# A two-layer decoder trunk: decay matrices and the D·x term moved to ScalarE, eight conditioning chunks moved from GpSimd to TensorE

## The chip, the cores and the metric

The kernel runs on one core of one Trainium2 chip. The metric is the device time of one execution in microseconds. A core has five engines, each with its own in-order queue: TensorE (PE, matrix products; PEld is its weight load), VectorE (DVE), ScalarE (ACT), GpSimd (POOL) and SyncE (SP, which here only issues DMAs). An instruction at the head of a queue that waits for another engine or for a DMA holds everything behind it on that queue. Instructions of different engines meet through semaphores.

## The reference, cut to what matters

512 tokens of width 1024 pass through two layers. All data are float32. The change touches layer 0's state-space part and its conditioning vector:

```python
cs = silu(c)
mod = cs @ ada_w[i] + ada_b[i]                    # 6*1024 values per layer: sh1, sc1, g1, sh2, sc2, g2
h = rms_norm(x, g) * (1 + sc1) + sh1
z, xbc, dt_raw, q, k, v = split(h @ w_in)
xbc = silu(causal_conv4(xbc)); xs, B, C = split(xbc)
a_cs = cumsum(dt * A)                             # within chunks of 128 tokens
decay = exp(where(causal, a_cs[l] - a_cs[s], -inf))
y_diag = einsum(((C @ B^T) * decay), xs * dt)     # per chunk, 32 heads of 64, 4 groups of 8 heads
y_off  = (C @ carried_state) * exp(a_cs)          # the state is carried from chunk to chunk
y = rms_norm((y_diag + y_off + D * xs) * silu(z)) # D is d_skip, one number per head
x = x + g1 * (concat(y, attention) @ w_out)
x = x + g2 * swiglu(rms_norm(x) * (1 + sc2) + sh2)
```

Layer 1 (a Conformer convolution and a second SwiGLU) and the final norm aren't touched.

## The kernel before, in words

**Products.** Activations lie with features on the 128 partitions and 512 tokens along the row. To keep float32 accuracy every weight and activation is split into a high part in a rounded type and the rest (`slab`, L179 to L196: the weight arrives by DMA in `raw`, ScalarE casts the high part `whi`, and the engine named by `eng` subtracts to get the low part `wlo`), and `products` (L198 to L211) adds three matmul passes: high·high (L207), low·high (L208), high·low (L210). `raw`, `whi` and `wlo` have two buffers each, so the next weight's DMA waits for the subtraction of the weight two before.

**Order.** The functions are written in program order, but the framework's scheduler lists the instructions of each engine's queue in an order of its own, from its estimates of when operands are ready. The queue is then fixed: at run time each engine goes through it in order.

**The state-space stage.** It runs from about 40 us to 415 us. For each of four groups, `ssm_inputs(g)` projects B, C (`wbc`, results `bc`), four x tiles (`wx`) and four z tiles (`wz`), through two PSUM banks named `pj` that are used in turn. `conv_tile` (L440) empties a bank: one ScalarE instruction (L443) and three VectorE ones (L446) that read PSUM, then a tanh (L449) and a product (L450). A bank is free again only after the last L446. `ssm_group(g)` then treats four chunks of 128 tokens: a broadcast DMA brings `ar` (eight heads by 128 positions of `a_cs`, on all partitions), GpSimd subtracts the per-partition `acs` (L487), VectorE takes the minimum with 0 (L488), ScalarE the exponential (L489), VectorE multiplies with the masked `cb` (L500), and TensorE forms `pd` (L504). From the second chunk on, `po` (L516) brings the carried state's part, times `ef` (exponential of another broadcast DMA, L513, L514); VectorE joins the two into `y1` (L517, L518). `pst` (L526) and `prev` (L529 to L532) carry the state; `btok` (L522), a ScalarE copy, feeds `pst`. After the four chunks VectorE adds D·x (L536), z is multiplied in (L537), and `ystat` collects squares. `ar` has two buffers, so the DMA for chunk c waits until `pd` of chunk c-2 has read its tile.

**Conditioning.** `mod` is needed in columns of 128. Sixteen chunks are made ahead of the stage by VectorE (`ada_wide`). The other 32 (`ada_pool`, L165 to L173) are made by GpSimd one at a time: a DMA of 128 columns, a product with `cs` (L170), three halving additions (L172), and a TensorE transpose with a VectorE sum (L153, L155, L156). Of these, eight are written behind each of groups 0 and 1, and the last 16 in the attention stage, three behind each head pair.

**Low parts in group 0.** `SL = (G, G, G, G)` (L179) gives the low parts of the dt, B/C and x weights of group 0 to GpSimd.

Of the kernel before, what the change touches and what calls it, by code (L numbers as in the profile page):

```python
# [9 lines left out]
F32 = mybir.dt.float32  # L10
F32R = mybir.dt.float32r
I32 = mybir.dt.int32
AF = mybir.ActivationFunctionType
ALU = mybir.AluOpType
# [3 lines left out]
P = 128  # L18
# [4 lines left out]
KT = D // P  # L23
# [3 lines left out]
GROUPS = 4  # L27
HEADS = 32
HPG = HEADS // GROUPS
# [48 lines left out]
def trunk_kernel(ctx: ExitStack, tc, a, out, dbg=None):  # L78
    nc = tc.nc
    V, S, G, PE = nc.vector, nc.scalar, nc.gpsimd, nc.tensor  # L80
# [5 lines left out]
    tmp = ctx.enter_context(tc.tile_pool(name="tmp", bufs=2))  # L86
# [3 lines left out]
    def bank(tag, name, shape=(P, T)):  # L90
        return psum.tile(list(shape), F32, tag=tag, name=name)
# [6 lines left out]
    ones = const.tile([P, P], F32, name="ones")  # L98
# [33 lines left out]
    cs = const.tile([P, KT], F32, name="cs")  # L132
# [11 lines left out]
    adab = [pa[:, 16:64], None]  # L144
# [3 lines left out]
    mod = [const.tile([P, 48], F32, name="mod0"), None]  # L148
# [9 lines left out]
    def ada_wide(pool, tag, l, j0, ws):  # L158
# [3 lines left out]
            V.scalar_tensor_tensor(acc, ws[k // 4][:, k % 4, :], cs[:, k:k + 1], acc, op0=ALU.mult, op1=ALU.add)  # L162
        return ada_finish(l, acc, j0, 4)

    def ada_pool(pool, bufs, l, j):  # L165
        w = pool.tile([P, 1024], F32, tag="adaw", name=f"adap{l}_{j}", bufs=bufs)
        G.dma_start(w.rearrange("p (k c) -> p k c", k=KT),
                          a["ada_w"][l][:, j * P:(j + 1) * P].rearrange("(k p) c -> p k c", p=P))
        w3 = w.rearrange("p (k c) -> p k c", k=KT)
        G.tensor_tensor(w3, w3, cs.unsqueeze(2).broadcast_to([P, KT, P]), op=ALU.mult)  # L170
        for n in (512, 256, 128):
            G.tensor_tensor(w[:, 0:n], w[:, 0:n], w[:, n:2 * n], op=ALU.add)  # L172
        ada_finish(l, w, j, 1)  # L173
# [2 lines left out]
        return [(l, j) for j in range(lo, hi)]  # L176


    SL = (G, G, G, G)  # L179

    def slab(parts, name, eng=V):

# [270 lines left out]
    def ssm_inputs(g):  # L453
# [19 lines left out]
                zs.append(z)  # L473
        return bt, ct, xs, zs

    ystat = Stat("ys", 16)

    def ssm_group(g, bt, ct, xs, zs):
        y1 = ssm.tile([P, 4, T], F32, tag="y1", name=f"y1_{g}", bufs=1)
        prev = None  # L480
        for c in range(NB):
            n = f"{g}_{c}"
            cl = slice(c * P, (c + 1) * P)
            hs = slice(c * HEADS + g * HPG, c * HEADS + (g + 1) * HPG)
            ar = ssm.tile([P, HPG, P], F32, tag="ar", name="ar" + n)
            nc.sync.dma_start(ar, a_dram[g * HPG:(g + 1) * HPG, c, :].unsqueeze(0).broadcast_to([P, HPG, P]))
            G.tensor_tensor(ar, ar, acs[:, hs].unsqueeze(2).broadcast_to([P, HPG, P]), op=ALU.subtract)  # L487
            V.tensor_scalar(ar, ar, 0.0, None, op0=ALU.min)  # L488
            S.activation(ar, ar, AF.Exp)  # L489
            px = bank(TB[0], "px" + n)  # L490
            for t in range(4):
                PE.transpose(px[:, t * P:(t + 1) * P], xs[t][:, cl], ident)
            xdt = ssm.tile([P, HPG, 64], F32, tag="xdt", name="xdt" + n)
            V.tensor_tensor(xdt, px.rearrange("p (h d) -> p h d", d=64),
                            dt[:, hs].unsqueeze(2).broadcast_to([P, HPG, 64]), op=ALU.mult)
            pb = bank(TB[1], "pb" + n, (P, 2 * P))
            PE.matmul(pb[:, 0:P], bt[:, cl], ct[:, cl], start=True, stop=True)
            cb = ssm.tile([P, P], F32, tag="cb", name="cb" + n)
            V.tensor_tensor(cb, pb[:, 0:P], tri, op=ALU.mult)
            V.tensor_tensor(ar, ar, cb.unsqueeze(1).broadcast_to([P, HPG, P]), op=ALU.mult)  # L500
            pd = bank(TB[2], "pd" + n)
            for hh in range(HPG):
                o = (hh % 2) * 64
                PE.matmul(pd[o:o + 64, (hh // 2) * P:(hh // 2 + 1) * P], xdt[:, hh, :], ar[:, hh, :],  # L504
                          start=True, stop=True)
            if c == 0:
                S.copy(y1[:, :, cl], pd.rearrange("p (t l) -> p t l", l=P))
            else:
                po = bank(TB[3], "po" + n)
                ef = ssm.tile([P, 4, P], F32, tag="xe", name="ef" + n, bufs=3)  # L510
                for e in range(2):
                    src = a_dram[g * HPG + e:(g + 1) * HPG:2, c, :]
                    nc.sync.dma_start(ef[e * 64:(e + 1) * 64], src.unsqueeze(0).broadcast_to([64, 4, P]))  # L513
                S.activation(ef, ef, AF.Exp)  # L514
                for t in range(4):
                    PE.matmul(po[:, t * P:(t + 1) * P], prev[:, 2 * t:2 * t + 2, :], ct[:, cl], start=True, stop=True)  # L516
                V.tensor_tensor(y1[:, :, cl], po.rearrange("p (t l) -> p t l", l=P), ef, op=ALU.mult)  # L517
                V.tensor_tensor(y1[:, :, cl], pd.rearrange("p (t l) -> p t l", l=P), y1[:, :, cl], op=ALU.add)  # L518
            if c < NB - 1:
                PE.transpose(pb[:, P:2 * P], bt[:, cl], ident)  # L520
                btok = ssm.tile([P, P], F32, tag="btok", name="btok" + n)
                S.copy(btok, pb[:, P:2 * P])  # L522
                xde = ssm.tile([P, HPG, 64], F32, tag="xe", name="xde" + n, bufs=3)
                G.tensor_tensor(xde, xdt, dend[:, hs].unsqueeze(2).broadcast_to([P, HPG, 64]), op=ALU.mult)
                pst = bank(TB[4], "pst" + n)
                PE.matmul(pst, btok, xde.rearrange("p h d -> p (h d)"), start=True, stop=True)  # L526
                new = ssm.tile([P, HPG, 64], F32, tag="prev", name="prev" + n)
                if c == 0:
                    S.copy(new, pst.rearrange("p (h d) -> p h d", d=64))  # L529
                else:  # L530
                    G.tensor_tensor(new, prev, cdec[:, hs].unsqueeze(2).broadcast_to([P, HPG, 64]), op=ALU.mult)
                    V.tensor_tensor(new, pst.rearrange("p (h d) -> p h d", d=64), new, op=ALU.add)  # L532
                prev = new
        for t in range(4):
            ft = 4 * g + t
            V.scalar_tensor_tensor(y1[:, t, :], xs[t], dsk[:, ft:ft + 1], y1[:, t, :], op0=ALU.mult, op1=ALU.add)  # L536
            (V if g == GROUPS - 1 else G).tensor_tensor(y1[:, t, :], y1[:, t, :], zs[t], op=ALU.mult)  # L537
            ystat.add(y1[:, t, :])
        nc.sync.dma_start(yd_dram[4 * g:4 * g + 4].rearrange("t p l -> p t l"), y1)

    jobs = [(0, j) for j in range(16, 48)]

    def ada_some(pool, bufs, n):
        for _ in range(min(n, len(jobs))):
            ada_pool(pool, bufs, *jobs.pop(0))
# [15 lines left out]
    nc.sync.dma_start(b_dram, bv)  # L561
    for g in range(GROUPS):
        ssm_group(g, *ins)
        if g < GROUPS - 2:
            ada_some(ssm, 2, 8)
        if g + 1 < GROUPS:
            ins = ssm_inputs(g + 1)
    ctx_s.close()
# [524 lines left out]
```

## Time and profile before

| | |
|---|---|
| time, median of 3 runs | 1872.89 us (1870.29 to 1874.12) |
| profiled execution | 1885.09 us, span 1882.8 us |
| PE busy | 1774.7 us, 94% |
| DVE busy | 1046.5 us, 56% |
| ACT busy | 693.1 us, 37% |
| POOL busy | 430.5 us, 23% |
| mean granted TensorE clock | 0.972 |
| chain that ended last | PE 73%, DVE 11%, DMA 7%, ACT 3%, POOL 2% |

The profiled execution is 12 us longer than the median run. "Busy" is a sum over the whole span, so it hides that the stages differ. The stage views below (busy time of each engine between two times) separate them. PE busy counts a matmul from its start to its modelled end; matmuls overlap, so the time that one takes from its neighbours is read from the distance between starts.

### The profile page before, as it was taken

Reading aid. Unit: us, or ns where it says so; the run is one execution under the profiler, and the core shown is the slowest. Engines: PE = TensorE matmul, PEld = TensorE weight load, DVE = VectorE, ACT = ScalarE, POOL = GpSimd, SP = SyncE. Lnnn points to the kernel's source line nnn. Section 1 sums busy time; section 2 is a strip of 40 time slices with the busy share of each in tenths; the row PEclk is TensorE's granted clock in tenths of the full one; section 3 lists DMA queues with packets and bytes.
Section 4 is the critical chain, followed back from the end, with each engine's and each line's share of the span. In section 5 each row is a group of like instructions: output and inputs, shape, how many; then the busy total and the mean of one; then the engine's idle time right before and its main releaser. Section 6 shows DMA issues by size and latency. Waiting matters only on the chain.

```text
span 1882.8 us, 24868 instructions
## 1 busy us (share of the span) xinstructions
PE 1774.7 (94%) x9735; PEld 1450.0 (77%) x9735; DVE 1046.5 (56%) x1978; ACT 693.1 (37%) x1331; POOL 430.5 (23%) x328
## 2 busy tenths in 40 slices
PE   5897978999999999997999999999999999999998
PEld 3676766777778878777888888897567988888888
DVE  7858687755565565558665664373204743333336
ACT  6333333334545454344421221253214632122225
POOL 1437686422443440003000000013020200000001
PEclk8998989999999999997999999999998999999999
DMA  8354454545444443424555553253640523322223
GB/s 301 102 138 140 141 141 134 137 112 152 123 128 149 133 125 122 124 74 141 181 190 190 188 201 114 79 169 80 180 132 1 169 77 102 101 89 93 87 94 130
DMA packets 232066, 247.84 MB, mean 132 GB/s; under 512 B 13946, under 2 KB 198076, under 8 KB 231949
## 3 DMA queue, kind: packets, MB, share of 16 engines
q1 hardware_dynamic: 220813, 204.31, 36.6%
q0 software_dynamic: 11136, 41.95, 6.8%
q8 instruction: 77, 1.26, 0.3%
q14 instruction: 40, 0.33, 0.1%
HBM read 228.73 MB, written 8.64 MB: 126 GB/s over the span
## 4 chain that ended last, share of the span: by engine, by line
PE 73%; DVE 11%; DMA 7%; ACT 3%; issue 2%; POOL 2%; SPq 1%; DVEq 0%; ACTq 0%; POOLq 0%
PE fd L207 4%; PE fd L208 4%; PE fd L210 4%; PE fg L208 4%; PE fg L207 4%; PE fu L207 4%; PE fu L208 4%; PE fu L210 4%; PE fg L210 4%; PE cps L959 2%; PE s L717 2%; DMA ar<-a_dram 2%; PE wa L207 1%; PE wa L208 1%; PE wa L210 1%
## 5 line engine op out<-in xcount | busy, mean ns | idle before, releaser
L249 POOL TENSOR_TENSOR n_acc<-n_acc,n_q 128x256 f32<-128x256 f32 x32 | 29.7, 929 | 561.8 <-ACT n_q L245 561.7
L207 PE MATMUL fd<-uh,wd_h 128*128 128x512 f32 (+1 forms) x448 | 148.6, 347 | 0.9 <-DVE xT L592 0.9
L195 DVE TENSOR_TENSOR wf_l<-wf_w,wf_h 128x1024 fp32r<-128x1024 f32 x88 | 106.1, 1241 | 74.4 <-ACT wf_h L194 74.4
L208 PE MATMUL fd<-uh,wd_l 128*128 128x512 f32 (+1 forms) x448 | 147.0, 344 | 0.0
L194 ACT CAST wf_h<-wf_w 128x1024 fp32r<-128x1024 f32 x88 | 87.7, 1048 | 115.7 <-PE fd L210 71.9
L208 PE MATMUL fg<-n_h,wf_l 128*128 128x512 f32 x320 | 126.1, 394 | 2.0 <-DVE wf_l L195 2.0
L207 PE MATMUL fg<-n_h,wf_h 128*128 128x512 f32 x320 | 126.3, 395 | 0.7 <-ACT wf_h L194 0.5
L208 PE MATMUL fu<-n_h,wf_l 128*128 128x512 f32 x320 | 124.7, 390 | 0.0
L207 PE MATMUL fu<-n_h,wf_h 128*128 128x512 f32 x320 | 124.6, 389 | 0.0
L172 POOL TENSOR_TENSOR adap<-adap 128x128 f32<-128x128 f32 (+2 forms) x96 | 103.5, 1082 | 4.7
L869 DVE TENSOR_TENSOR fs<-fs,fu 128x512 f32<-128x512 f32 x40 | 27.5, 688 | 130.2 <-PE fu L210 130.2
L743 ACT ACTIVATE s<-s,nm 128x128 f32<-128x128 f32 x192 | 79.4, 415 | 50.7 <-DVE nm L739 40.4
L194 ACT CAST wd_h<-wd_w 128x1024 fp32r<-128x1024 f32 (+1 forms) x64 | 57.1, 941 | 101.2 <-PE fd L210 80.6
L592 DVE SCALAR_TENSOR_TENSOR xT<-fd,mod,xT 128x512 f32<-128x512 f32 (+1 forms) x64 | 39.1, 615 | 98.1 <-PE fd L210 97.8
L207 PEld LDWEIGHTS fd<-uh,wd_h 128*128 128x128 f32 x448 | 84.1, 188 | 12.0 <-DVE xT L592 1.3
L208 PEld LDWEIGHTS fd<-uh,wd_l 128*128 128x128 f32 x448 | 84.2, 188 | 10.5
L210 PE MATMUL fd<-ul,wd_h 128*128 128x512 f32 (+1 forms) x448 | 91.9, 343 | 0.0
L170 POOL TENSOR_TENSOR adap<-adap,cs 128x1024 f32<-128x1024 f32 x32 | 67.6, 2112 | 90.3 <-DMA adap<-in_ada_w 90.2
L195 DVE TENSOR_TENSOR wd_l<-wd_w,wd_h 128x1024 fp32r<-128x1024 f32 (+1 forms) x64 | 67.7, 1090 | 34.7 <-ACT wd_h L194 34.4
L162 DVE SCALAR_TENSOR_TENSOR adaa<-adaw,cs,adaa 128x512 f32<-128x512 f32 x112 | 84.8, 758 | 2.6
L210 PEld LDWEIGHTS fd<-ul,wd_h 128*128 128x128 f32 x448 | 72.9, 188 | 10.6
L210 PE MATMUL fg<-n_l,wf_h 128*128 128x512 f32 x320 | 79.1, 389 | 0.0
(400 smaller groups left out, 4584.5 us busy)
## 6 DMA issues: line engine op xcount, KB each, us to landing
adaw<-in_ada_w POOLq DMA_DIRECT2D x24, 1024.0 KB, 5.7
wf_w<-in_ffn_w_gate SPq DMA_DIRECT2D x22, 1024.0 KB, 5.2
wf_w<-in_ffn_w_up SPq DMA_DIRECT2D x22, 1024.0 KB
adap<-in_ada_w POOLq DMA_DIRECT2D x32, 512.0 KB, 5.5
wd_w<-in_ffn_w_down SPq DMA_DIRECT2D x16, 1024.0 KB, 5.1
wd_w<-in_ffn_w_down SPq DMA_DIRECT2D x16, 768.0 KB, 4.6
wa_w<-in_hy_w_out SPq DMA_DIRECT2D x20, 512.0 KB, 4.1
u<-cu SPq DMA_DIRECT2D x128, 67.5 KB, 2.0
```

Source lines behind the costliest of these rows:

```text
L162: V.scalar_tensor_tensor(acc, ws[k // 4][:, k % 4, :], cs[:, k:k + 1], acc, op0=ALU.mult, op1=ALU.add)
L170: G.tensor_tensor(w3, w3, cs.unsqueeze(2).broadcast_to([P, KT, P]), op=ALU.mult)
L172: G.tensor_tensor(w[:, 0:n], w[:, 0:n], w[:, n:2 * n], op=ALU.add)
L194: S.copy(hi[:, s:e], raw[:, s:e])
L195: eng.tensor_tensor(lo[:, s:e], raw[:, s:e], hi[:, s:e].bitcast(F32), op=ALU.subtract)
L207: PE.matmul(ps[:, cols], hi[:, o(k):o(k) + P], xh, start=k == 0, stop=False)
L208: PE.matmul(ps[:, cols], lo[:, o(k):o(k) + P], xh, start=False, stop=False)
L210: PE.matmul(ps[:, cols], hi[:, o(k):o(k) + P], acts[k][1][:, cols], start=False, stop=k == nk - 1)
L592: V.scalar_tensor_tensor(xT[m][:, cols], ps[:, cols], mod[l][:, go + m:go + m + 1], xT[m][:, cols], op0=ALU.mult, op1=ALU.add)
L717: marks[hp, 0] = marks[hp, 1] = PE.matmul(ps[:, o:o + 2 * wd].rearrange("p (e w) -> p e w", e=2), q, k, start=True, stop=True)
L743: S.activation(s[:, o:o + wd], s[:, o:o + wd], AF.Exp, bias=nm, accum_out=l)
L959: PE.matmul(ps[g * 32:(g + 1) * 32, :], w4[k][:, g * 8 + m, :], u4[k][:, g, t:t + w], start=m == 0, stop=m == 7)
```

## The change: three moves

- **Decay.** `ar` is no longer subtracted on GpSimd and clamped on VectorE. ScalarE forms Relu(acs - ar), head by head in eight instructions of 128x128 (the bias is one number per partition, so it differs by head), and then exp of the negative.
- **D·x.** ScalarE writes D·x into `y1` before the chunks; VectorE adds `pd` to it in every chunk (before: a ScalarE copy of `pd` in the first chunk, an addition in the others), and GpSimd adds `po`·`ef`. The four VectorE additions at the group's end are gone.
- **Conditioning and low parts.** Chunks 16 to 23 are made by TensorE (`ada_rows`): eight 128x512 weight tiles through three buffers, each multiplied with a stationary operand of 32 columns of which one is `cs`, into one of four 32-row quarters of a PSUM bank; a ScalarE copy; four products with ones that add the rows. Chunks 24 to 47 all go to the attention stage on GpSimd, still three per head pair, so all eight pairs have some (before, the 16 there were used up in the sixth). The low parts of group 0's B/C and x weights go to VectorE.

```diff
+    def ada_rows(pool, l, j0):
+        ps = bank("C", f"adar{l}_{j0}")
+        for k in range(KT):
+            w = pool.tile([P, 512], F32, tag="adaw", name=f"adaw{l}_{j0}_{k}", bufs=3)
+            nc.sync.dma_start(w, a["ada_w"][l][k * P:(k + 1) * P, j0 * P:j0 * P + 512])
+            PE.matmul(ps[k % 4 * 32:(k % 4 + 1) * 32, :], cs32[:, k, :], w, start=k < 4, stop=k >= 4)
+        rw = tmp.tile([P, 512], F32, tag="st_sq", name=f"adas{l}_{j0}")
+        S.copy(rw, ps)
+        pm = bank("C", f"adac{l}_{j0}", (P, 4))
+        for j in range(4):
+            PE.matmul(pm[:, j:j + 1], rw[:, j * P:(j + 1) * P], ones[:, 0:1], start=True, stop=True)
+        V.tensor_tensor(mod[l][:, j0:j0 + 4], pm, adab[l][:, j0:j0 + 4], op=ALU.add)
...
-    SL = (G, G, G, G)
+    SL = (G, V, V, V)
...
+    cs32 = ssm.tile([P, KT, 32], F32, name="cs32", bufs=1)
+    V.memset(cs32, 0.0)
+    V.tensor_copy(cs32[:, :, 0], cs)
...
         y1 = ssm.tile([P, 4, T], F32, tag="y1", name=f"y1_{g}", bufs=1)
+        for t in range(4):
+            S.mul(y1[:, t, :], xs[t], dsk[:, 4 * g + t:4 * g + t + 1])
...
-            G.tensor_tensor(ar, ar, acs[:, hs].unsqueeze(2).broadcast_to([P, HPG, P]), op=ALU.subtract)
-            V.tensor_scalar(ar, ar, 0.0, None, op0=ALU.min)
-            S.activation(ar, ar, AF.Exp)
+            for hh in range(HPG):
+                S.activation(ar[:, hh, :], ar[:, hh, :], AF.Relu, scale=-1.0, bias=acs[:, hs.start + hh:hs.start + hh + 1])
+            S.activation(ar, ar, AF.Exp, scale=-1.0)
...
-            if c == 0:
-                S.copy(y1[:, :, cl], pd.rearrange("p (t l) -> p t l", l=P))
-            else:
+            V.tensor_tensor(y1[:, :, cl], pd.rearrange("p (t l) -> p t l", l=P), y1[:, :, cl], op=ALU.add)
+            if c > 0:
...
-                V.tensor_tensor(y1[:, :, cl], po.rearrange("p (t l) -> p t l", l=P), ef, op=ALU.mult)
-                V.tensor_tensor(y1[:, :, cl], pd.rearrange("p (t l) -> p t l", l=P), y1[:, :, cl], op=ALU.add)
+                V.tensor_tensor(ef, po.rearrange("p (t l) -> p t l", l=P), ef, op=ALU.mult)
+                G.tensor_tensor(y1[:, :, cl], ef, y1[:, :, cl], op=ALU.add)
...
-            ft = 4 * g + t
-            V.scalar_tensor_tensor(y1[:, t, :], xs[t], dsk[:, ft:ft + 1], y1[:, t, :], op0=ALU.mult, op1=ALU.add)
...
-    jobs = [(0, j) for j in range(16, 48)]
+    jobs = [(0, j) for j in range(24, 48)]
...
-        if g < GROUPS - 2:
-            ada_some(ssm, 2, 8)
+        if g < 2:
+            ada_rows(ssm, 0, 16 + 4 * g)
```

The scheduler lists all queues anew. Line numbers of the changed kernel are 14 to 18 higher. On ScalarE, this stood between the first chunk of group 0 and the group's third (`wx_0_h` is a weight cast for group 1, `sb` the emptying of the bank of group 1's B):

```order
L194 CAST wx_0_h<-wx_0_w 128x1024 x2
L507 COPY y_0_843<-pd_0_861 128x4x128
L529 COPY prev_0_878<-pst_0_876 128x512
L514 ACTIVATE ef_2_954<-ef_2_954 128x512
L489 ACTIVATE ar_2_927<-ar_2_927 128x1024
L522 COPY btok_1_918<-pb_1_892 128x128
L443 ACTIVATE sb_1169<-bc_0_1119,cbh,cwh 128x512
```

Now the same place reads (`sc` is the bank of group 1's C, the `ar_0` at the end is group 1's first chunk):

```order
L507 ACTIVATE ar_2_947<-ar_2_947,acs 128x128 x8
L532 ACTIVATE ef_2_981<-ef_2_981 128x512
L508 ACTIVATE ar_2_947<-ar_2_947 128x1024
L540 COPY btok_1_938<-pb_1_911 128x128
L457 ACTIVATE sb_1152<-bc_0_1102,cbh,cwh 128x512
L463 ACTIVATE th_1157<-sb_1152 128x512
L540 COPY btok_2_992<-pb_2_965 128x128
L507 ACTIVATE ar_3_1001<-ar_3_1001,acs 128x128 x8
L508 ACTIVATE ar_3_1001<-ar_3_1001 128x1024
L532 ACTIVATE ef_3_1035<-ef_3_1035 128x512
L507 ACTIVATE ar_0_1449<-ar_0_1449,acs 128x128 x8
L457 ACTIVATE sc_1160<-bc_1_1103,cbh,cwh 128x512
```

The eight Relu instructions of a chunk stand ahead of `btok` and of the instructions that empty the projection banks, and they are the first on ScalarE to need the `ar` DMA.

On VectorE, at the end of group 0 (`cb_0`, `ar_0` and the `sx` from `x_1_0` belong to group 1), before:

```order
L450 SCALAR_TENSOR_TENSOR sx_1251<-th_1256,sx_1251 128x512
L536 SCALAR_TENSOR_TENSOR y_0_843<-sx_608,dsk,y_0_843 128x512
L536 SCALAR_TENSOR_TENSOR y_0_843<-sx_616,dsk,y_0_843 128x512
L536 SCALAR_TENSOR_TENSOR y_0_843<-sx_682,dsk,y_0_843 128x512
L536 SCALAR_TENSOR_TENSOR y_0_843<-sx_690,dsk,y_0_843 128x512
L488 TENSOR_SCALAR ar_1_1498<-ar_1_1498 128x1024
L499 TENSOR_TENSOR cb_0_1476<-pb_0_1474,cst 128x128
L446 SCALAR_TENSOR_TENSOR sx_1317<-x_1_0_1267,cwh,sx_1317 128x511
```

and now:

```order
L209 TENSOR_TENSOR wz_0_l<-wz_0_w,wz_0_h 128x1024
L464 SCALAR_TENSOR_TENSOR sx_1234<-th_1239,sx_1234 128x512
L518 TENSOR_TENSOR cb_0_1469<-pb_0_1467,cst 128x128
L460 SCALAR_TENSOR_TENSOR sx_1300<-x_1_0_1250,cwh,sx_1300 128x511
L519 TENSOR_TENSOR ar_0_1449<-ar_0_1449,cb_0_1469 128x1024
```

The four D·x additions and the clamp are gone from in front of `cb_0` and the bank-emptying `sx`.

On TensorE, behind the third chunk of group 0 (`bc` and `x` are the projections of group 1), before:

```order
L504 MATMUL pd_2_944<-ar_2_927,xdt_2_937 64x128 x8
L516 MATMUL po_2_953<-sc_542,prev_1_924 128x128 x4
L526 MATMUL pst_2_969<-xde_2_967,btok_2_965 128x512
L497 MATMUL pb_3_986<-sc_542,sb_534 128x128
L153 MATMUL ada_16_1036<-cst,adap_16_1030 128x128
L208 MATMUL x_0_0_1193<-n_h_242,wx_0_l 128x512
```

and now:

```order
L523 MATMUL pd_2_970<-ar_2_947,xdt_2_963 64x128 x8
L534 MATMUL po_2_980<-sc_545,prev_1_944 128x128 x4
L544 MATMUL pst_2_996<-xde_2_994,btok_2_992 128x512
L516 MATMUL pb_3_1019<-sc_545,sb_537 128x128
L171 MATMUL adar_16_1060<-adaw_16_0_1061,cs_474 32x512
L171 MATMUL adar_16_1060<-adaw_16_1_1064,cs_474 32x512
L171 MATMUL adar_16_1060<-adaw_16_2_1067,cs_474 32x512
L225 MATMUL bc_1_1103<-n_l_309,wbc_h 128x512
```

The eight quarter-column products of a set stand as three, three, one and one in the queue, the second three 25 projection products, `pd_3` and `po_3` behind the first. The chunk now comes one C product and three x products earlier among the projections.

## Rows read from the trace of the kernel before

**Rows 1.** Stages: us, length, busy PE, PEld, DVE, ACT, POOL, then granted clock
```profile
95.00:415.00 320.00, 286.02 (x1472) 227.23 (x1471) 228.39 (x278) 111.15 (x161) 185.35 (x130) 0.94 0.49 132
440.00:860.00 420.00, 403.84 (x2154) 323.75 (x2154) 238.01 (x697) 190.91 (x544) 114.36 (x92) 0.98 0.43 123
1000.00:1150.00 150.00, 150.00 (x672) 123.65 (x671) 91.22 (x122) 34.90 (x42) 8.98 (x12) 1.00 0.55 182
148.00:151.00 3.00, 3.00 (x9) 2.28 (x8) 3.00 (x6) 0.54 (x1) 2.84 (x3) 0.52 0.31 65
```

**Rows 2.** Waits of PE, 95 to 415 us: total, times, longest
```profile
PE z L207 <- DVE sx L446: 12.1, 2, 9.0
PE pb L520 <- DVE cb L499: 5.3, 1, 5.3
PE pb L497 <- DVE xdt L494: 4.1, 2, 3.2
PE ada L153 <- POOL adap L172: 3.8, 1, 3.8
PE pst L526 <- ACT btok L522: 3.4, 2, 2.4
```

**Rows 3.** Waits of PE, 40 to 95 us
```profile
PE x L207 <- DVE sc L446: 4.3, 1, 4.3
PE x L208 <- POOL wx_l L195: 4.0, 2, 3.3
```

**Rows 4.** DVE groups by line, 95 to 415 us: busy, mean ns, idle before
```profile
L500 DVE TENSOR_TENSOR ar<-ar,cb 128x1024 f32<-128x1024 f32 x16 | 24.2, 1514 | 0.6 <-ACT ar L489 0.5
L195 DVE TENSOR_TENSOR wz_l<-wz_w,wz_h 128x1024 fp32r<-128x1024 f32 x14 | 22.6, 1612 | 0.0
L488 DVE TENSOR_SCALAR ar<-ar 128x1024 f32<-128x1024 f32 x16 | 20.1, 1257 | 23.0 <-POOL ar L487 23.0
L536 DVE SCALAR_TENSOR_TENSOR y<-sx,dsk,y 128x512 f32<-128x512 f32 x16 | 18.3, 1206 | 0.0
```

**Rows 5.** Timeline of DVE, then PE, at group 0's end: start us, us, instruction
```profile
165.93 5.84 DVE L536 SCALAR_TENSOR_TENSOR y<-sx,dsk,y 128x512 f32<-128x512 f32 x4
173.36 0.28 DVE L499 TENSOR_TENSOR cb<-pb,cst 128x128 f32<-128x128 f32 x1
...
173.70 0.48 PE L520 MATMUL pb<-cst,sb 128*128 128x128 f32 x1 [5.31 <-DVE cb L499]
```

**Rows 6.** Timeline of DVE, then POOL, ahead of the stage
```profile
66.83 2.50 DVE L413 SCALAR_TENSOR_TENSOR dt_acc<-dt_acc,dt_w 128x128 f32<-128x128 f32 x1
73.32 0.29 DVE L414 SCALAR_TENSOR_TENSOR dt_acc<-dt_acc,dt_w 128x128 f32<-128x128 f32 x1
...
66.80 4.72 POOL L195 TENSOR_TENSOR wx_l<-wx_w,wx_h 128x1024 fp32r<-128x1024 f32 x2
```

**Rows 7.** ACT groups by line, 40 to 430 us
```profile
L514 ACT ACTIVATE ef<-ef 128x512 f32<-128x512 f32 x12 | 7.6, 632 | 44.5 <-DMA ef<-a_dram 44.5
L743 ACT ACTIVATE s<-s,nm 128x128 f32<-128x128 f32 x1 | 0.4, 402 | 6.1 <-DVE nm L739 6.1
L406 ACT ACTIVATE dt_e<-dt_e 128x128 f32<-128x128 f32 x1 | 0.3, 311 | 0.0
```

**Rows 8.** Chain that ended last: broadcast DMAs on it, start us, us
```profile
204.06 8.24 DMA ar<-a_dram
290.42 5.94 DMA ar<-a_dram
```

**Rows 9.** PE groups: convolution of layer 1, then 95 to 415 us; timeline of row sums
```profile
L959 PE MATMUL cps<-u,w 128*32 128x512 f32 x256 | 29.3, 594 | 0.0
...
L526 PE MATMUL pst<-xde,btok 128*128 128x512 f32 x24 | 13.6, 650 | 3.4 <-ACT btok L522 3.4
L153 PE MATMUL ada<-cst,adap 128*128 128x128 f32 x16 | 4.5, 281 | 4.7 <-POOL adap L172 3.8 <-DVE prev L532 0.9
...
419.70 0.95 PE L256 MATMUL ys_s<-ones,ys_acc 128*128 128x1 f32 x8
```

## The prediction

> **What bounds the kernel now.** I read the stage views first, then who waits for whom inside the stage that the change touches, then single instructions.
>
> The stages differ [rows 1]. The feed-forward stretch (1000 to 1150 us) has PE busy all the time at full clock. The attention stage (440 to 860) has PE busy 403.8 of 420 us, clock 0.98. The state-space stage (95 to 415) has 286.0 of 320 us, so 34.0 us of idle PE, and a granted clock of 0.94. So PE bounds all three, but only here can time be had without taking work off PE.
>
> The clock is a second loss. After an idle PE of 2.9 us the stretch 148 to 151 runs at 0.52 [rows 1], the 1.2 GHz level, with PE busy throughout. A mean of 0.94 over 320 us is 19 us of full-rate time, but part of it falls on idle time; I take two thirds, 13 us, as lost while PE worked. That is an estimate.
>
> What PE waits for [rows 2]: VectorE ended 21.5 us of the waits shown (12.1 + 5.3 + 4.1), GpSimd's conditioning 3.8, ScalarE's `btok` 3.4; smaller ones make up the 34. VectorE is busy 228 of 320 us, GpSimd 185, ScalarE 111 [rows 1]. Group 0's end shows how it comes about [rows 5]: four D·x additions hold VectorE from 165.93 for 5.84 us, behind them stand the clamp and `cb`, and PE waits 5.31 us for `cb`. No operand was late; the queue was full.
>
> VectorE is also slow. The same subtraction and product of 128x1024 average 1.61 and 1.51 us here, D·x of 128x512 averages 1.21 [rows 4]. Ahead of the stage it is plainer [rows 6]: one 128x128 step takes 2.50 us while GpSimd subtracts a low part, and the like step takes 0.29 us once GpSimd is done. So GpSimd's work costs VectorE time as well as its own.
>
> **The change part by part.**
>
> *Decay to ScalarE.* Gone: 16 clamps on VectorE, 20.1 us [rows 4], and 16 GpSimd subtractions. New on ScalarE: 8 Relu of 128x128 per tile. The nearest rows are 0.31 us (no per-partition bias) and 0.40 us (bias and a row sum) [rows 7], so 2.5 to 3.2 us a tile; ours has the bias but no row sum, and I take the middle, 2.8. Sixteen tiles are 45 us on an engine with 209 us free [rows 1]. What hides them is that free time, as long as ScalarE isn't waiting at the head of its queue (second rival).
>
> *D·x to ScalarE, `po` to GpSimd.* Gone: 16 VectorE additions, 18.3 us [rows 4], and four ScalarE copies. New: 16 ScalarE scalings near 0.63 us (a 128x512 row [rows 7]), 10 us; four more VectorE additions, under 5 us at D·x's own price; 12 GpSimd additions, which GpSimd has room for once its conditioning is gone.
>
> *Low parts to VectorE.* Six subtractions, 6 x 1.61 = 9.7 us at most [rows 4], less with GpSimd quiet. On the other side PE's 4.0 us wait for GpSimd's `wx_l` goes, and most of its 4.3 us wait for `sc` [rows 3], which had its cause in the slow steps of rows 6. I leave 1 us of that wait, and charge 1 us because `wbc_l` now stands before the sum that releases the first activations: 8.3 - 2 = 6.3 us gained ahead of the stage.
>
> *Conditioning to TensorE.* Sixteen products of 32 columns by 512. From below: the convolution, which runs four column quarters beside each other, does 128 such products (256 records) in 29.3 us, 0.23 each. From above: a 128-column float32 product of the same length is 13.6 / 12 = 1.13 us [rows 9]. Each of the two sets stands as three, three, one and one, so there are four triples and four singles. A lone one can't overlap a partner and is nearest to `pst`, 1.13 us. A triple lies in three different quarters, as in the convolution, and I take one `pst` for it. Eight times 1.13 is 9.0 us; ends 3.7 and 18. The row sums: two times four products, 0.95 us per four [rows 9], 1.9 us. Against it 16 transposes of 0.28 us leave the stage, 4.5 us at most [rows 9]; they overlap neighbours, so I count 2. Net +8.9 us of PE. Eight chunks come back in the attention stage, where GpSimd has 306 of 420 us free [rows 1]; with their transposes and the slower VectorE I charge 1 us.
>
> *What the waits become.* Available in the stage: 34 + 13 = 47 us. VectorE sheds 38 us and its slow-down, so I expect the density of the attention stage, the other stage with much VectorE and ScalarE work between products [rows 1]: 16.2 us idle and two thirds of 8.4 us of clock per 420 us, which is 16.6 us per 320. To that I add 5 us for ScalarE at the three group changes. There `btok` and the emptying of the banks stand behind Relu. The `ar` tile lands 5.9 to 8.2 us after `pd` has freed its buffer [rows 8]; then come 2.8 for Relu, 0.63 for `ef` [rows 7] and some 1.1 for the exponential of twice that length, so `btok` is ready 10.4 to 12.7 us after `pd`. PE, with 33 projection products at 150 / 672 = 0.223 us [rows 1] and `pst`, `pd` and `po` of about 1.1 us each [rows 9] between, wants it after 10.8. So a wait of 0 to 2 us each time, where 3.4 us in all stand now [rows 2]. Left: 22 of 47, a gain of 25.
>
> *Sum*, against the profiled execution of 1885.1 us: -25 - 6.3 + 8.9 + 1 = -21.4, so 1863.7. The median run is 12.2 us shorter with the same program; I carry the difference over: 1872.9 - 21.4 = 1851.
>
> **Rivals.**
>
> *The stage becomes dense.* If VectorE was the only cause, the stage goes toward the feed-forward stretch [rows 1], with 3 us left instead of 22: -44 - 6.3 + 9.9 = -40, 1832. For it: VectorE ends most waits [rows 2]. Against: the carried state still goes through PE, ScalarE, GpSimd and VectorE in turn, in every chunk. 17%.
>
> *ScalarE's queue becomes the bound: slower.* ScalarE already waits 44.5 us for `ef` at the head of its queue [rows 7], harmlessly, as little stood behind. Now each `ar` DMA can do the same, and `btok`, `sb`, `sc` stand behind. At the group changes twelve tiles lie so (the next group's first tiles included). If each holds PE 3 us, that is 36 us, with the clock in its present proportion (47 per 34) 50 us, on top of the 17 of the attention density: 67 left instead of 47, so +20 - 6.3 + 9.9 = +23, 1896. It decides where the loss left passes 43 us, that is 27 us of new loss or 1.6 us of PE wait per tile. Against: the chain from DMA to the masked product loses an engine, GpSimd, and a hop. 10%. The Trainium skill, "ScalarE: Activation LUTs", section "Rules for kernel authors", speaks for this rival: relu and min belong on VectorE, not on ScalarE. By its figures there for an instruction with a pointer bias (section "What ACT_TABLE_LOAD costs": 280 ns + 0.833 ns per element, 93 ns overlapped) a tile's Relu would be 2.4 us, an estimate. No row here shows a plain Relu; VectorE's clamp is 1.26 us [rows 4], so by engine time alone the rule agrees with the trace.
>
> *PE waits for the new weight tiles.* With three buffers the second triple's DMAs can't start before the first triple is read, and then stand behind an `ar` DMA on SP; only 25 projection products, `pd` and `po` lie between, about 8 us, against a landing in 5.9 to 8.2 us for the transfers of rows 8, which are twice as large. Up to 4 us per set for the triple and 2 for the singles, 12 us with the clock added: 1864. 15%.
>
> *Nothing moves.* The waits return elsewhere and eat the gain: 1873. 4%.
>
> **How the numbers follow.** Forecast 54%, dense 17%, weight tiles 15%, ScalarE 10%, nothing 4%. The forecast's own range is 1840 to 1862. I give 1830 to 1870, which leaves out the far half of the dense case and the ScalarE case. A difference below 0.2%, 3.7 us, can't be told from none here: faster takes the first three cases but for a few per cent, 0.84; same 0.06; slower 0.10.
>
> **What would show it.** Right: between the start of the first `ar` DMA and the attention stage PE idle falls from 34 to near 17 us, and its clock rises to 0.97 or more; `wz_l` and `ar`·`cb` on VectorE fall toward 1.25 us; no PE wait on `cb` or on `sx` above 3 us; the quarter-column products hold PE near 1.1 us per group. Wrong: ScalarE waits for `ar` DMAs of some 5 us each with PE waits on `btok` or on `sc` behind them (second rival), or PE waits at the quarter-column products ended by DMA `adaw` (third). The forecast fails if the stage keeps more than 40 us of idle and clock loss, or if attention grows by more than 4 us.

## The result, and the profile after

| | before | after |
|---|---|---|
| time, median (4 runs each) | 1871.72 us (1870.29 to 1874.12) | 1846.74 us (1844.22 to 1851.72) |
| ratio, 95% interval | | 0.9862 [0.9839, 0.9886] |
| profiled execution, span | 1882.8 us | 1842.5 us |
| mean granted TensorE clock | 0.972 | 0.983 |

The kernel became 1.4% faster, 25 us. The forecast was 1851 us with 1830 to 1870. The time came out as forecast, but two of the terms did not, and they lie on opposite sides: the state-space stage gained more, and the attention stage lost 6 to 8 us where 1 had been priced.

Busy time by stage after, with the columns of [rows 1]; the first row is the window in which the stage of before lay, the second the attention:

```profile
95.00:415.00 320.00, 312.02 (x1665) 244.72 (x1664) 192.64 (x302) 176.21 (x364) 90.43 (x63) 0.99 0.50 136
440.00:860.00 420.00, 393.40 (x2152) 321.14 (x2151) 256.93 (x686) 186.17 (x509) 168.14 (x137) 0.96 0.46 134
```

In the first, idle PE fell from 34.0 to 8.0 us and the clock rose from 0.94 to 0.99, while ScalarE's busy time rose from 111 to 176 us. In the second PE lost 10 us of busy time, 393.4 for 403.8, and the clock fell from 0.98 to 0.96. (After, the attention starts some 40 us sooner, so the second window holds other work and the two rows can't be set against each other. Cut at the same events, as in the table further down, the attention has the same PE busy time, 454.7 us before and 454.9 after, at a clock of 0.97 both times; its idle PE rose from 21.9 to 27.8 us. In e8, the second trace of before, it is 451.6 us busy at 0.98 and 22.7 idle.)

The waits of PE after: first from 95 to 415 us, answering [rows 2], then from 440 to 830 us (total, times, longest).

```profile
PE x L221 <- DVE sc L460: 6.5, 3, 2.3
PE z L221 <- DVE sx L460: 0.9, 1, 0.9
PE pst L544 <- ACT btok L540: 0.5, 1, 0.5
...
PE ada L153 <- POOL adap L186: 10.2, 2, 7.7
PE s L733 <- DVE m L736: 3.6, 3, 2.6
```

Of the VectorE waits of [rows 2], `z` on `sx` fell from 12.1 to 0.9 us, and those of `pb` on `cb` (5.3) and on `xdt` (4.1) have gone. What is left is the emptying of a bank, `x` on `sc`, in three short waits, one at each group change. Two of them begin on ScalarE. ACT, DVE and PE at the first (start us, us):

```profile
132.35 2.45 ACT L507 ACTIVATE ar<-ar,acs 128x128 f32<-128x128 f32 x8 [2.95 <-DMA ar<-a_dram]
134.71 0.76 ACT L457 ACTIVATE sc<-bc,cbh,cwh 128x512 f32<-128x512 f32 x1
...
135.50 1.53 DVE L460 SCALAR_TENSOR_TENSOR sc<-bc,cwh,sc 128x511 f32<-128x511 f32 x2 [6.65 <-ACT sc L457]
...
138.97 0.47 PE L221 MATMUL x<-n_h,wx_h 128*128 128x512 f32 x1 [2.04 <-DVE sc L460]
```

ScalarE waits 2.95 us for the `ar` DMA and works 2.45 us on the Relus; only then does it start on the bank of `sc`, for which VectorE has been idle 6.65 us, and PE waits 2.04 (a subtraction of 1.2 us that VectorE does between its steps on `sc` adds to it). At the second change it is the same, 2.93 us for the DMA and 2.25 of PE. At the third, 2.2 us, `sc` was late in VectorE's own queue. The wait for a conditioning chunk has moved from the stage into the attention and is larger there, 10.2 for 3.8 us. It stands in two places at the attention's end, the last two chunks. PE there, then GpSimd:

```profile
803.26 0.28 PE L222 MATMUL wa<-ath,wa_l 128*128 128x256 f32 x1
811.28 0.48 PE L153 MATMUL ada<-cst,adap 128*128 128x128 f32 x1 [7.74 <-POOL adap L186]
...
825.56 0.42 PE L153 MATMUL ada<-cst,adap 128*128 128x128 f32 x1 [2.49 <-POOL adap L186]
...
766.31 3.48 POOL L186 TENSOR_TENSOR adap<-adap 128x512 f32<-128x512 f32 x3
...
798.80 0.93 POOL L181 DMA_DIRECT2D adap<-in_ada_w  x1 [17.29 <-PE wy L222]
806.33 1.89 POOL L184 TENSOR_TENSOR adap<-adap,cs 128x1024 f32<-128x1024 f32 x1 [6.61 <-DMA adap<-in_ada_w]
```

GpSimd had finished the third chunk from the end at 769.8 us, but PE's queue came to its transpose only at 797.91. Until then the one buffer was taken, so the next chunk's DMA started at 798.80.

VectorE after, 95 to 415 us (busy, mean ns, idle before), answers [rows 4]; the clamp and D·x are no longer among its groups:

```profile
L519 DVE TENSOR_TENSOR ar<-ar,cb 128x1024 f32<-128x1024 f32 x16 | 22.2, 1388 | 0.3
L209 DVE TENSOR_TENSOR wz_l<-wz_w,wz_h 128x1024 fp32r<-128x1024 f32 x12 | 16.3, 1356 | 0.0
L525 DVE TENSOR_TENSOR y<-pd,y 128x512 f32<-128x512 f32 x16 | 11.0, 685 | 11.4 <-PE pd L523 11.3
```

The product fell from 1514 to 1388 ns and the subtraction from 1612 to 1356 without being changed. ScalarE, 40 to 430 us, and PE's new groups, 95 to 415 us:

```profile
L507 ACT ACTIVATE ar<-ar,acs 128x128 f32<-128x128 f32 x128 | 39.2, 389 | 32.9 <-DMA ar<-a_dram 27.3 <-issue 5.5
L498 ACT ACTIVATE y<-sx,dsk 128x512 f32<-128x512 f32 x16 | 11.1, 719 | 2.4 <-DVE sx L464 2.4
...
L171 PE MATMUL adar<-adaw,cs 128*32 128x512 f32 x32 | 8.4, 604 | 0.0
L176 PE MATMUL adac<-ones,adas 128*128 128x1 f32 x16 | 1.9, 239 | 0.0
```

ScalarE does wait for the `ar` DMAs, 27.3 us in all. No PE wait above 0.5 us hangs on `btok`, but the two on `sc` described above, 4.3 us, do hang on it. The quarter-column products don't wait for their weights (idle before: 0.0).

### The profile page after: what moved, and what is told of

Same layout as the page of the kernel before. It is cut to its first block, busy times and chain, and to the rows that moved or that the text cites. A ratio compares the mean times of both kernels' runs of the same rounds, so it can differ in the third digit from the quotient of the medians.

```text
span 1842.5 us, 25006 instructions
## 1 busy us (share of the span) xinstructions
PE 1764.2 (96%) x9775; PEld 1438.8 (78%) x9775; DVE 999.3 (54%) x1944; ACT 740.7 (40%) x1473; POOL 347.6 (19%) x278
## 4 chain that ended last, share of the span: by engine, by line
PE 83%; DVE 6%; DMA 5%; ACT 2%; issue 1%; POOL 1%; SPq 0%; DVEq 0%; ACTq 0%; POOLq 0%
PE fd L221 4%; PE fd L222 4%; PE fd L224 4%; PE fg L222 4%; PE fu L221 4%; PE fg L221 4%; PE fu L222 4%; PE fu L224 4%; PE fg L224 4%; PE cps L975 3%; PE s L733 2%; DMA ar<-a_dram 2%; PE z L221 2%; PE z L222 2%; PE z L224 2%; PE qq L221 2%
## 5 line engine op out<-in xcount | busy, mean ns | idle before, releaser
L222 PEld LDWEIGHTS fd<-uh,wd_l 128*128 128x128 f32 x448 | 84.2, 188 | 10.5
L884 ACT ACTIVATE fs<-fg 128x512 f32<-128x512 f32 x40 | 23.9, 598 | 146.7 <-PE fg L224 146.7
L186 POOL TENSOR_TENSOR adap<-adap 128x512 f32<-128x512 f32 (+2 forms) x72 | 79.1, 1099 | 5.0
L224 PE MATMUL fu<-n_l,wf_h 128*128 128x512 f32 x320 | 79.1, 389 | 0.0
```

Of the source, the lines that this page charges most:

```text
L222: PE.matmul(ps[:, cols], lo[:, o(k):o(k) + P], xh, start=False, stop=False)
L224: PE.matmul(ps[:, cols], hi[:, o(k):o(k) + P], acts[k][1][:, cols], start=False, stop=k == nk - 1)
```

## Where the time went, by events

For every kernel below the profiled execution is cut at three PE events: the first product of x, the first `o` of the attention, the first feed-forward product `fg`. All in us. The second execution of before (e8) lies near its median; the one that the prediction used was 12 us longer, about 5 of them in the stage.

| kernel | to first x | x to `o` (stage) | `o` to `fg` (attention) | rest | span |
|---|---|---|---|---|---|
| before, as predicted from | 58.0 | 381.6 | 476.6 | 966.6 | 1882.8 |
| before, second execution (e8) | 57.5 | 376.7 | 474.3 | 962.7 | 1871.2 |
| after | 58.1 | 341.0 | 482.7 | 960.7 | 1842.5 |
| e1 decay and D·x | 57.5 | 364.4 | 472.8 | 966.7 | 1861.4 |
| e2 D·x alone | 57.7 | 384.5 | 466.7 | 962.9 | 1871.8 |
| e3 conditioning alone | 59.0 | 366.2 | 490.0 | 969.4 | 1884.6 |
| e4 low parts alone | 63.9 | 370.0 | 469.1 | 963.1 | 1866.1 |
| e5 four chunks a pair | 59.0 | 341.1 | 506.4 | 962.4 | 1868.9 |
| e6 clamp on VectorE | 59.5 | 355.8 | 485.7 | 962.1 | 1863.1 |
| e7 all four groups' rows | 58.1 | 355.4 | 466.9 | 963.7 | 1844.1 |
| e9 three groups' rows | 58.7 | 346.0 | 470.3 | 964.8 | 1839.8 |
| e10 low parts on GpSimd | 59.2 | 343.7 | 480.7 | 961.9 | 1845.5 |
| e11 without two chunks | 58.4 | 342.4 | 477.2 | 968.6 | 1846.6 |

Against e8 the change gains 35.7 us in the stage, loses 8.4 in the attention and 0.6 at the start and gains 2.0 later: the sum is 28.7. The last column but one spreads over almost 9 us among kernels that are alike there, so single traces can't tell less than some 4 us a column; times and intervals are used for verdicts. Two more cautions. The executions traced aren't all ordinary: e3's took 11.7 us more than the median of e3's runs, e4's and e10's 6.1 and 5.5 less than theirs; the other changed kernels' lie within 3 us. And the cut at `o` moves a little with the order of the queue: 16 products of the next head pairs more stand before it in e2 than after, 4 more before the change, 7 more in e7 and e9, at some 0.23 us each.

## The experiments

Theory 1 is that PE in the stage waited for VectorE's own queue. Theory 2 is that VectorE was held up by GpSimd's conditioning. A median is given with the ratio to before, measured beside it, and its 95% interval.

**e1, decay and D·x to ScalarE, the rest as before; e2, D·x alone.** e1 is the parts of the diff at the `ar` tile and at `y1`, e2 only the latter:

```
+        for t in range(4):
+            S.mul(y1[:, t, :], xs[t], dsk[:, 4 * g + t:4 * g + t + 1])
...
-            ft = 4 * g + t
-            V.scalar_tensor_tensor(y1[:, t, :], xs[t], dsk[:, ft:ft + 1], y1[:, t, :], op0=ALU.mult, op1=ALU.add)
```

> The kernel before with the state-space moves alone (decay matrices and D*x on ScalarE, po's addition on GpSimd); conditioning and low parts stay on GpSimd. Theory 1 (VectorE's own queue was the cause; the change takes 38 us of instructions off it): most of the gain, -14 us, about 1858, and the PE waits on cb and sx at the group changes (8.4 and 9.0 us) gone. Theory 2 (GpSimd's conditioning slows VectorE and that was the cause): little, -5 us, about 1867, with wz_l and ar*cb still near 1.5 us.

> The kernel before with only D*x on ScalarE and po's addition on GpSimd; the decay stays on GpSimd and VectorE. Theory 1: the four additions of 5.8 us ahead of cb go, -7 us, about 1865. Theory 2: -2 us. If the decay is what counts, this one does next to nothing and e1 has the gain.

e1: 1861.07 us, 0.9930 [0.9903, 0.9957]. e2: 1870.91, 0.9973 [0.9954, 0.9992]. So the two moves are worth some 13 us, about half of the change, as theory 1 had it; of them D·x alone is 4 or 5 (by its interval 1.5 to 8.6), and the rest, 8 to 10, comes with the decay matrices. D·x alone doesn't empty the queue that [rows 5] show: PE's waits from 95 to 415 us in e2 are

```profile
PE x L221 <- DVE sc L460: 12.0, 3, 5.7
PE z L221 <- DVE sx L460: 8.5, 1, 8.5
```

The wait on `cb` went, and the same engine is waited for at the next bank instead.

**e3, conditioning alone; e4, low parts alone.** e3 is `ada_rows` with its call and operand and the shorter list of chunks for GpSimd, e4 one line, `SL = (G, V, V, V)`.

> The kernel before with only the conditioning moved (eight chunks on TensorE in quarters, chunks 24 to 47 in the attention stage). Theory 1: VectorE keeps its 38 us, PE gets 8 us more work and the attention stage its new waits on GpSimd (10 us), so no gain: -2 to +4 us, about 1873. Theory 2: VectorE's instructions fall toward 1.25 us, PE idle in the stage falls by 15 us or more, net -10 us, about 1862.

> The kernel before with only the low parts of group 0's B/C and x weights on VectorE. Both theories: the 4.0 us PE wait on wx_l goes. Theory 1: most of the 8.3 us ahead of the stage goes, -5 us, about 1867. Theory 2: GpSimd still does two conditioning chunks there, VectorE stays slow and has six more instructions, the wait on sc grows: 0 to +3 us.

e3: 1874.65, 1.0006 [0.9984, 1.0028]. e4: 1873.92, 0.9994 [0.9977, 1.0011]. Neither moves the time, and yet both shorten the stage, by 10.5 and 6.7 us against e8. What eats the gain differs. In e3 it is the attention, 15.7 us longer, though part of that may belong to an execution 11.7 us over its median. The wait at its end is the one of after (PE, 780 to 900 us):

```profile
PE ada L153 <- POOL adap L186: 9.5, 2, 6.1
```

In e4 it is the start, 6.4 us later; with the 6.7 of the stage that leaves nothing (the shorter attention of this trace goes with its short execution). There two low parts on VectorE fall together with GpSimd's first chunks. VectorE, GpSimd and PE of e4 (start us, us):

```profile
55.30 5.13 DVE L195 TENSOR_TENSOR wx_l<-wx_w,wx_h 128x1024 fp32r<-128x1024 f32 x2
...
53.33 3.80 POOL L170 TENSOR_TENSOR adap<-adap,cs 128x1024 f32<-128x1024 f32 x2 [3.44 <-DMA adap<-in_ada_w]
57.09 6.65 POOL L172 TENSOR_TENSOR adap<-adap 128x512 f32<-128x512 f32 x6
...
63.87 0.76 PE L207 MATMUL x<-n_h,wx_h 128*128 128x512 f32 x1 [5.05 <-DVE sb L446]
```

and the same two instructions after, where GpSimd has nothing to do between 38.7 and 102.9 us:

```profile
52.70 2.35 DVE L209 TENSOR_TENSOR wx_l<-wx_w,wx_h 128x1024 fp32r<-128x1024 f32 x2
...
58.08 0.47 PE L221 MATMUL x<-n_h,wx_h 128*128 128x512 f32 x1 [0.28 <-DVE sb L460]
```

5.13 us beside GpSimd's conditioning, 2.35 without: the low parts can pay only if the conditioning leaves as well, and by e10 below that they pay even then isn't shown. This is theory 2, and e3 shows it on an instruction that no part of its diff touches: the clamp of 128x1024, 95 to 415 us, first in e8, then in e3.

```profile
L488 DVE TENSOR_SCALAR ar<-ar 128x1024 f32<-128x1024 f32 x16 | 20.5, 1282 | 22.0 <-POOL ar L487 22.0
```
```profile
L505 DVE TENSOR_SCALAR ar<-ar 128x1024 f32<-128x1024 f32 x15 | 14.1, 939 | 25.6 <-POOL ar L504 25.6
```

Single instructions tell it more sharply than means. Of e8's 16 clamps, the 5 with no GpSimd instruction beside them took 0.69 or 0.70 us, and the 7 with one beside them for over 80% of their time took 0.93 to 2.37. In e3, 12 of 16 ran alone, in 0.67 to 0.70 us. The product with `cb` took 1.21 to 1.23 us whenever it ran alone, in e8 and after alike.

In the stage the parts nearly add up: e1, e3 and e4 shorten it by 12.3, 10.5 and 6.7 us, 29.5 in all, and the change by 35.7. What doesn't add up is the start: e4's 6.4 us aren't there in the change. These two differences, 6.2 and some 6 us, are about what the change gains beyond e1.

**e5, four chunks a pair in the attention.** This was to end the conditioning before the last pair.

```
-        ada_some(att, 1, 3)
+        ada_some(att, 1, 4)
```

> The changed kernel with four conditioning chunks behind each head pair instead of three, so that all 24 are done in six pairs, as the 16 of before were. Theory (the new PE waits of 7.7 and 2.5 us for GpSimd stand at chunks 46 and 47, behind the last pair, where the queue has little other work to give them time): -8 us, about 1838. Rival (GpSimd is late in any place, at some 14 us a chunk): the waits move to earlier pairs, 1844 to 1850.

1869.02 us, 0.9989 [0.9971, 1.0007]: nearly all of the gain gone, where I had expected more of it; neither forecast holds. The attention is 23.7 us longer than after. The last chunks are no longer waited for; the order is what changed. PE, GpSimd, DVE and PE of e5 at the second pair (start us, us):

```profile
459.67 0.27 PE L153 MATMUL ada<-cst,adap 128*128 128x128 f32 x1
459.78 0.60 PE L772 MATMUL pt<-cst,s 128*128 128x128 f32 x4
...
447.56 1.29 POOL L767 TENSOR_TENSOR s<-s 128x512 f32<-128x512 f32 x1
...
468.92 0.28 DVE L800 COPY wr<-wt 16x128 f32<-16x128 f32 x1 [0.48 <-PE wt L798]
...
481.68 2.08 PE L733 MATMUL s<-kz,q 128*128 128x256 f32 x4 [5.93 <-DVE at L821]
```

and of after, PE and DVE at the same place:

```profile
447.91 0.60 PE L772 MATMUL pt<-cst,s 128*128 128x128 f32 x4
...
461.22 0.28 DVE L800 COPY wr<-wt 16x128 f32<-16x128 f32 x1 [2.85 <-PE wt L798]
```

GpSimd's sum of the exponentials `s` was done by 448.9 us in e5 too, but in PE's queue the first `pt` transposes now stood behind a second chunk's, with 11 us of value products ahead of both. So `wr` is 7.7 us late (1.0 of it from an attention that started later), and with it the weights' trip through DRAM (`wr`, `w_dram`, `at`), and PE waits 5.9 us for `at`; another pair has 6.7 us of the same. These two are 12.6 of the 23.7 us; the rest lies in many smaller waits and isn't settled.

**e6, the clamp on VectorE.** After, with subtraction and minimum in one VectorE instruction per head instead of Relu on ScalarE.

```
-                S.activation(ar[:, hh, :], ar[:, hh, :], AF.Relu, scale=-1.0, bias=acs[:, hs.start + hh:hs.start + hh + 1])
-            S.activation(ar, ar, AF.Exp, scale=-1.0)
+                V.tensor_scalar(ar[:, hh, :], ar[:, hh, :], acs[:, hs.start + hh:hs.start + hh + 1], 0.0, op0=ALU.subtract, op1=ALU.min)
+            S.activation(ar, ar, AF.Exp)
```

> The changed kernel with the subtraction and the clamp of the decay on VectorE (eight 128x128 instructions per tile with a per-partition number) in place of the eight Relu on ScalarE; nothing goes back to GpSimd. Theory (VectorE is the engine that is late): 128 more VectorE instructions of about 0.25 us, 30 us, bring the waits on cb, sc and sx back, +8 us, about 1855. Rival (VectorE has room once GpSimd is quiet, and ScalarE's head-of-queue waits for ar are what is left): 1842 to 1847.

1864.08 us, 0.9958 [0.9939, 0.9978], 17 us over after, more than the 8 or so that I had expected. The new group is VectorE's costliest in the stage (84 to 390 us):

```profile
L507 DVE TENSOR_SCALAR ar<-ar,acs 128x128 f32<-128x128 f32 x128 | 45.4, 422 | 23.6 <-DMA ar<-a_dram 23.5
```

The stage is 14.8 us longer than after's. VectorE now has 45.4 us more work in it, and it is also the engine that waits for the DMA at the head of its queue, 23.5 us, with the sums that empty PE's banks behind it. Both speak for the first theory; how much each costs this run doesn't separate. On ScalarE the like wait, 27.3 us, left 4.3 us of PE waits behind it.

**e7, e9, e11: what the wait at the attention's end is worth.** e7 makes 16 chunks by rows, four behind each of the groups 0 to 3, and leaves 16 for GpSimd; e9 does so behind three groups and leaves 20; e11 is after without the product of the last two chunks. The edit of e9 (in e7 the numbers are 32 and 4; in e11 the first is `range(24, 46)` and the last two columns are copied from the bias):

```
-    jobs = [(0, j) for j in range(24, 48)]
+    jobs = [(0, j) for j in range(28, 48)]
...
-        if g < 2:
+        if g < 3:
```

> The changed kernel with 16 chunks on TensorE, four behind every group, and only chunks 32 to 47 on GpSimd in the attention stage. Theory: 8 us more of PE, 10 us of waits for GpSimd gone, one us of transposes gone: -3 us, about 1844, no clear gain. Rival (weight tiles in three buffers hold PE up in the later groups, where SP's queue is fuller): 1855.

> The changed kernel with a third group's row sums on TensorE: 12 chunks in quarter-columns, 20 left for GpSimd in the attention (three per pair, so that the seventh pair takes the last two and the eighth none). Theory 1, the wait of 10.2 us on chunks 46 and 47 at the attention's end hides the last pair's own chain (ScalarE's ath, VectorE's atl and xT), which showed 4.6 + 1.2 + 1.0 us of TensorE waits once those chunks had gone from there: about 3.4 us come back and 4 chunks cost 4.75 - 1.1 = 3.6 us of TensorE, 1847 us, with no wait on adap at the end and one of some 4.6 us on ath. Theory 2, the wait on adap is lost in full and nothing stands behind it: 10.2 - 3.6, 1840 us.

> The changed kernel without the conditioning product of chunks 46 and 47 (their columns hold the bias alone). Theory 1, behind the wait on adap stands the last pair's own chain: of 10.2 us some 3 to 4 come back, 1843 us. Theory 2, the wait is lost in full: 1836 us.

e7: 1846.95 us, 0.9871 [0.9847, 0.9895]. e9: 1843.73, 0.9825 [0.9801, 0.9850]. e11: 1846.67, 0.9840 [0.9815, 0.9866]. (e9, e10 and e11 stand beside runs of before with a median of 1876.43.) In all three the 10.2 us on `adap` have gone from the end of the attention, and in all three another wait has come out from under it. PE of e11, 780 to 900 us:

```profile
PE wa L221 <- ACT ath L827: 4.4, 1, 4.4
PE f_a L221 <- ACT n_h L322: 3.4, 1, 3.4
PE wa L221 <- DVE xT L609: 1.6, 4, 0.6
PE n_s L270 <- ACT n_q L259: 1.6, 1, 1.6
```

The last pair's own result `ath` is late by 4.4 us, as it is in e7 (4.6), e9 (4.5) and was in e8 (4.5). The attention of e11 is 5.5 us shorter than after's, half of the wait, and its idle PE is 22.5 us, nearly the 21.9 of before. The time is 0.2% lower by ratio, inside the interval. So theory 1 of e9 and e11 holds in the attention; that the time gains by it isn't shown. e7 gains 15.8 us in the attention against after and pays 14.4 in the stage, of which its two further row sets are some 10, as the two of after took 8.4 + 1.9 us, and 7 products that moved ahead of the cut 1.6. e9 pays 5.0 for 12.4 and is the fastest kernel measured here; its interval and after's overlap, so that it beats after is not shown, that it beats before is.

**e10, low parts back on GpSimd**, those of x, of which the expectation speaks, and those of B/C.

```
-    SL = (G, V, V, V)
+    SL = (G, G, G, G)
```

> The changed kernel with the low parts of x's weights back on GpSimd. Theory 1, the parts gain in the stage one by one (low parts alone shortened first x to norm sums by some 7 us): the stage grows from 319.5 to about 326 us and the time is 1853 us. Theory 2, GpSimd has room for them once the conditioning and the decay matrices are gone: no change, 1847 us.

1852.77 us, 0.9889 [0.9861, 0.9916]. By ratio 0.3% slower than after, 5 us, with overlapping intervals; the stage is 2.7 and the start 1.1 us longer. The forecast of 1853 fits, that of no change isn't excluded; the trace, of an execution 5.5 us below the median, can't decide it. e10 is also e1 with the conditioning moved, so before, e1, e10 and after form a ladder: 13 us for decay and D·x, some 8 more for the conditioning (by ratio 0.4%), some 5 more for the low parts. The intervals of neighbours overlap on the last two steps, so only their sum, 12 us, is clear of noise.

**e8, before a second time**, for a trace of an ordinary execution:

> The kernel before, unchanged, for a second trace: the first profiled execution took 1885 us, 12 us more than the median. If the 12 us lie in the state-space stage, PE idle there is nearer 25 us than 34 in an execution of median length, and the gain from the change shown by the first pair of traces (40 us) is too large by that much. If they lie elsewhere, the stage reads the same.

1873.4 us, span 1871.2 us: 11.6 us shorter than the first trace. In the table 4.9 of them lie in the stage, 2.3 in the attention and 3.9 behind; no single wait explains them. PE idle from 95 to 415 us is 31.9 us, for 34.0 in the first.

## Why the prediction was right, and where it was not

- *What bounds the stage.* Right. VectorE's queue and GpSimd's hold on VectorE were both at work, as e1 and e6 show for the one and e3 and e4 for the other. The signs named came: clock 0.99, `cb` not waited for, `z` on `sx` below 1 us. `wz_l` fell to 1356 ns and `ar`·`cb` to 1388, not quite to 1250: 9 of the 16 products still had GpSimd at work beside them, and the 7 that ran alone took 1.21 to 1.23 us.
- *What is left in the stage: 22 of 47 us.* Mis-sized. 8.0 us of idle and, by the prediction's own two thirds, 2 of clock are left, so 37 us came instead of 25. The 5 us at the three group changes came, 6.5 us, though on `sc` and not on `btok`, and 4.3 of them begin on ScalarE. What was too large is the 16.6 us taken from the attention's density: beyond the group changes only 3.5 us are left. With 10 us left in all the stage came nearer to the first rival's dense case (3) than to the forecast (22).
- *Ahead of the stage: 6.3 us.* The waits of [rows 3] fell from 8.3 to under 1 us (0.4 on `draw`, 0.3 on `sb`), a little more than priced. The price was right, the cause was not: the term credited the move of the low parts, but with the low parts still on GpSimd and only the conditioning gone the same waits are 1.5 us (e3) and 0.7 (e10), and with the low parts moved and the conditioning still there, 5.5 (e4).
- *PE's new work: 8.9 us.* Right: 8.4 and 1.9 us busy against 9.0 and 1.9 forecast; the 2 us taken off for the transposes no run measures. A triple in three quarters of the columns takes as long as a single:

```profile
126.67 1.06 PE L171 MATMUL adar<-adaw,cs 128*32 128x512 f32 x6
...
146.22 1.04 PE L171 MATMUL adar<-adaw,cs 128*32 128x512 f32 x2
```

- *Relu 2.8 us a tile.* It took 39.2 / 16 = 2.45, below my lower end; D·x took 0.72 us, not 0.63. Neither decided anything.
- *The attention: +1 us.* This step failed. The attention is 6.1 us longer than in the table's first row and 8.4 longer than in e8. I had priced the eight chunks by GpSimd's free time, and it has enough of it. But a chunk is a chain, a DMA into one buffer, GpSimd, a transpose at a fixed place in PE's queue, the next DMA, and three a pair now run to the very end. The lines above show it: a finished chunk waits 28 us for its transpose, and the next one is late by that. By e11 the last two links are worth 5.5 us of the attention. "Attention grows by more than 4 us" was one of the signs by which I said the forecast would fail; it came, and the time held because the stage gave 12 us more than asked. That the sum came within 5 us of the time is in this part luck.
- *The difference of 12.2 us carried over.* Some 5 us of it lay in the stage, so part of the gain read from that trace was not there in an ordinary run. The 40.3 us between the two profiled spans are 28.7 against e8 and 25 between medians.
- *The rivals.* ScalarE's queue: the waits on `ar` came (27.3 us), and with them PE waits on `sc`, as the rival had said, but only two, 4.3 us in all, where it had asked for 3 us at each of twelve tiles. The page's rule that relu and min belong on VectorE (the Trainium skill, "ScalarE: Activation LUTs", "Rules for kernel authors") does not hold here: in e6's form, eight instructions a tile with the subtraction in them, following it costs 17 us. There the Trainium skill gives the rule with a figure for bf16. These data are float32, and engine time hardly differs, 389 ns for the Relu and 422 for the clamp. What differs is which engine PE waits for. PE on the weight tiles: no wait. (That rival's 12 us were the waits alone; with the clock in the prediction's proportion, 47 per 34, it would have been 17 and 1868.)

## What to carry to other kernels

Price a moved instruction by who waits for the engine that it joins: the same clamps, with 39 us of work and 27 of waiting on ScalarE or 45 and 24 on VectorE, make 17 us of difference in the kernel's time. Work handed to an idle engine as a chain of single steps needs its end looked at, not its sum: the last link was waited for 10 us, and making the chain end earlier (e5) changed the order of other work and lost 22 us. Parts that each measure zero alone can be worth 12 us together on top of a third; read where each one's gain went before dropping it.

## What the runs showed of the hardware

- Two VectorE subtractions of 128x1024 took 5.13 us while GpSimd worked on the conditioning and 2.35 us while it was idle; a VectorE clamp of one input fell from a mean of 1282 to 939 ns when only the conditioning had left (e8, e3). Alone it took 0.69 or 0.70 us, beside GpSimd's work 0.93 to 2.37 (e8).
- Three float32 products of 32 columns by 512, in three quarters of the columns, took 1.06 us together, and one alone 1.04.
- Per head of 128x128, subtraction and clamp in one instruction took 0.42 us on VectorE (e6) and 0.39 us on ScalarE as a Relu with a per-partition bias (after).
